# A decoder layer on one core: the first up-projection group also as seven products, and the norm's sums and scaling one group later

## The chip, the cores and the metric

The kernel runs on one core of one Trainium2 chip. The metric is the device time of one execution in microseconds; the median of several runs counts. Everything below is single-core, and the granted clock of the matrix engine in the profiled execution was 0.999 of full speed.

## The reference

One decoder layer on 512 tokens of width 1024, all in float32. Cut to what the change touches, the layer ends like this:

```python
x = x + jnp.einsum('bsd,de->bse', merged, w_out[l])        # 1024 x 1024
h2 = rmsnorm(x, norm_mlp_g[l])
up = jnp.square(jax.nn.relu(jnp.einsum('bsd,df->bsf', h2, w_up[l])))   # 1024 -> 4096
x = x + jnp.einsum('bsf,fd->bsd', up, w_down[l])           # 4096 -> 1024
```

Ahead of that lie a first RMS norm, one combined projection, differential attention, a gated linear recurrence and a gated merge of both branches. The change leaves their arithmetic alone.

## The kernel before, in words

**Splitting.** Each operand is split in two float32r parts: ScalarE copies it to `whi` (or the first half of an activation tile), VectorE subtracts that from the original and gets `wlo`. Every product is three matmuls: high by high, high by low, low by high. So each weight block of 128 x 1024 costs one DMA of 512 KB, one ScalarE cast and one VectorE subtraction before TensorE can use it. `cast_hi` and `cast_lo` (L1029 to L1057) do this for the last stage, `ahead` (L1059) calls them a step in advance. ScalarE and VectorE work strictly in the order in which the code issues their instructions (`InOrder`, L59).

**Weight buffers.** Four pairs `whi`/`wlo` go round, and every fifth unit of the last stage (L1035, `own`) has a pair of its own in the pool `fin`, which is opened when the pools of the middle stages close (L902). `fin` takes over their memory.

**The last stage** (L904 on) starts with the w_out projection in four pieces (`merged`, L929): each piece adds the residual into `x2`, multiplies with the gain into `q`, splits `q` into the tile `h2` (four forms), builds four sums of quarters (`sums`, L940, four more forms in `h2`), and squares `x2` for the norm. The norm's factor is not applied to `h2`: since relu squared passes it through, it is applied to `x2` instead.

**Up and down.** The 4096 hidden columns are cut into eight groups of 512. Odd groups (and, before the change, group 0) are computed plainly: kind `pl`, four weight blocks `b0`, `b2`, `b1`, `b3`, each block 24 matmuls of 512 columns. Groups 2, 4 and 6 are kind `up`: a 2 x 2 block product in seven products `M1` to `M7` (Winograd's form of Strassen), each 24 matmuls of 256 columns, in the order M1, M5, M6, M2, M7, M3, M4 (L957). M1, M6, M7 and M4 accumulate in one PSUM bank (Y), M5 and M3 in another (Z), M2 in a third (X); between them ScalarE or VectorE take the bank's state out (`up_out`, L1112): after M1 a copy `snap`, after M5 and M6 copies into `q`, after M2, M7 and M3 additions or subtractions. After every two groups come the seven products of the down projection, twice (kind `dn`). The list `steps` (L959 to L973) holds this order.

**Weight sums.** M5, M6, M7 and M4 of an `up` group need sums of weight blocks. `weight_sums` (L281) makes them on the DMA engines during the recurrence: GpSimd issues a load of one block into the tile `sum`, then a load that adds the next block, then a store to DRAM, ten DMAs a group one after another, since all go through the one tile. The tile lies in pool `stg`, at byte 225,248 to 229,344 of each partition. In `fin` the low half of the fifth unit's own pair (`wlo`) lies at 224,896 to 229,248, so the first instruction that writes it waits for the last of the weight sums' DMAs. In the kernel before, the fifth unit is block `b0` of group 1.

**The norm.** `sums2` (L1205) splits the sum of squares, `norm2` (L1208) adds it over the partitions with two matmuls, puts the result in `r2`, and schedules eight multiplications of `x2` with `r2`; they come before the first addition of a down product into `x2`. Calls put off by `later` run when a running estimate of TensorE's time (`tick`) has passed their due time.

Of the kernel before, what the change touches and what calls it, by code (L numbers as in the profile page):

```python
# [11 lines left out]
F32 = mybir.dt.float32  # L12
# [7 lines left out]
P = 128  # L20
# [17 lines left out]
def tile_block(ctx: ExitStack, tc: tile.TileContext, x, w_in, w_rga, w_rgx, w_pa, w_pr, w_o,  # L38
# [237 lines left out]
    tgr, tga = [None] * KT, [None] * KT  # L276
    es_act = ExitStack()
    stg = es_act.enter_context(tc.tile_pool(name="stg", bufs=1, side="right"))
    summed = [{p: dp.tile([P, 1024], F32, name=f"up{n}{p}") for p in ("M5", "M7", "M6", "M4")} for n in range(2, 8, 2)]

    def weight_sums(behind):  # L281
        t = stg.tile([P, 1024], F32, name="sum")
        G.tensor_copy(t[:, :1], behind[:, :1])
        for n in range(2, 8, 2):
            for blocks in (((0, None), (1, "M5"), (3, "M6"), (2, "M4")), ((1, None), (3, "M7"))):
                for b, p in blocks:
                    if p:
                        G.dma_start(t, w_up[n, b], accum_op=ALU.add)
                        G.dma_start(summed[n // 2 - 1][p], t)
                    else:  # L290
                        G.dma_start(t, w_up[n, b])

# [668 lines left out]
    def products(kind, a, order=ORDER7, first=3, lead=()):  # L961
        steps.extend((kind, a, p, q) for q in (range(first), range(first, 4)) for p in lead)
        steps.extend((kind, a, p, every) for p in order if p not in lead)

    I = InOrder(nc.tensor)
    for d in range(4):
        if d:
            products("up", 2 * d)
        else:
            products("pl", 0, ("b0", "b2", "b1", "b3"))  # L970
        products("pl", 2 * d + 1, ("b0", "b2", "b1", "b3"))
        products("dn", (d, 0))
        products("dn", (d, 1))  # L973
# [4 lines left out]
    for kind, a, p in ops:  # L978
        if kind == "pl":
            loads.append(((kind, a, p), w_up[a, int(p[1])]))  # L980
        elif kind == "up":
            loads.append(((kind, a, p), w_up[a, int(uses[p][0][1])] if p in ("M1", "M2", "M3") else summed[a // 2 - 1][p]))
# [76 lines left out]
    def ahead():  # L1059
        if half:  # L1060
            cast_lo()
        if can_cast():
            cast_hi()
# [11 lines left out]
    def later(us, f):  # L1075
        due.append((clk[0] + us, f))
# [128 lines left out]
    def sums2():  # L1205
        split(s2[:, 0], s2[:, 1], ssq)
# [10 lines left out]
    for j in range(4):  # L1217
        if j == 2:
            wb.raws = 2
        for n, _ in enumerate(merged(j)):  # L1220
            load()
            while late and n == 1:
                late.pop(0)()
            if j == 3 and n == 0:
                ahead()
                ahead()
            while owing and n == 0:
                owing.pop(0)()
    slots[0] += 1
    ahead()  # L1230
    ahead()
    owing.pop(0)()
    while late:
        late.pop(0)()
    later(3.0, owing.pop(0))
    later(6.0, lambda: late.pop(0)())
    seen, banks = {}, {}
    ACT8 = {"M1": 0, "M4": 3, "M2": 2, "M5": 4, "M6": 5, "M7": 6, "M3": 7}
    for n, (kind, a, p, pairs) in enumerate(steps):
        o = kind, a, p  # L1240
        if (kind, a) not in banks:
            banks[kind, a] = [psum("acc") for _ in range(4 if kind == "pl" else 3)]
            if kind == "dn" and a[0] == 3:
                banks[kind, a][1] = banks[kind, a][1], psum("acc")
        while n_low[0] <= number[o]:
            if half:
                cast_lo()
            else:
                assert can_cast()
                cast_hi()  # L1250
        hi, lo = units[number[o]]
        if kind == "pl":
            oc, kc = int(p[1]) % 2, int(p[1]) // 2
            ps = banks[kind, a][2 * oc:2 * oc + 2]
            for m in range(8):
                u, i = (m // 4, m % 4) if kc else (m % 2, m // 2)
                for e, (l, r) in enumerate(((hi, 0), (hi, 1), (lo, 0))):
                    I.matmul(ps[u], l[:, i, P * u:P * u + P], h2[:, r, i, 2 * kc:2 * kc + 2], start=kc == i == e == 0, stop=kc == 1 and i == 3 and e == 2)
                if m == 7:
                    finish(o)  # L1260
                if kc and i == 3:
                    plain_out(a, oc, u, ps[u])
                tick(0.68)
                if m % 4 == 3:
                    ahead()
            if n in (1, 3):
                sums2() if n == 1 else norm2()
            continue
        X, Y, Z = banks[kind, a]
        b = {"M2": X, "M5": Z, "M3": Z}.get(p, Y)  # L1270
        f = FORM[p]
        k = seen.get(o, 0)
        seen[o] = k + len(pairs)
        parts = [slice(u, u + 1) for u in range(2)] if isinstance(b, tuple) else [slice(0, 2)]
        if kind == "dn" and a[1] == 0 and p == "M1" and k == 0:
            I.matmul((b[0] if isinstance(b, tuple) else b)[:, :64], hi[:, 0, :P], forms[2 * a[0]][:, 0, f, 0, :64], start=True, stop=True)
        for u in range(2):
            d = b[u][:, :256] if isinstance(b, tuple) else b[:, 256 * u:256 * u + 256]
            for z, i in enumerate(pairs):
                for e, (l, r) in enumerate(((hi, 0), (hi, 1), (lo, 0))):  # L1280
                    act = h2[:, r, i, ACT8[p]] if kind == "up" else forms[2 * a[0] + i // 2][:, r, f, i % 2]
                    I.matmul(d, l[:, i, P * u:P * u + P], act, start=p in ("M1", "M2", "M5") and k == z == e == 0 and (u == 0 or isinstance(b, tuple)),
                             stop=i == 3 and e == 2, skip_group_check=True)
            if seen[o] == 4 and kind == "up" and u == 1:
                up_out(a, p, X, Y, Z)
            elif seen[o] == 4 and kind == "dn" and (len(parts) == 2 or u == 1):
                down_out(a, p, X, Y, Z, parts if len(parts) == 1 else parts[u:u + 1])
            if u == 0:
                tick(0.355 * len(pairs))
        if seen[o] == 4:  # L1290
            finish(o)
        if kind == "dn" and a[1] == 0 and p == "M2":
            if half:
                cast_lo(False)
        else:
            ahead()
        tick(0.355 * len(pairs))
# [43 lines left out]
```

## Time and profile before

| what | value |
|---|---|
| median of 3 runs | 856.3 us (854.63 to 857.79) |
| the profiled execution, its own time | 855.89 us |
| its span in the profile | 854.1 us |
| busy: TensorE / VectorE / ScalarE / GpSimd | 847.6 / 627.9 / 448.8 / 85.3 us |
| w_out projection | 486.95 to 530.46 us |
| groups 0 and 1, both plain, with the norm's two matmuls | 530.46 to 574.50 us |
| two down halves and group 2 | 574.50 to 631.90 us |
| group 3, plain | 631.90 to 653.70 us |

Times in the trace are counted from the start of the span. PE is TensorE, DVE is VectorE, ACT is ScalarE, POOL is GpSimd, SP the engine that issues most DMAs. Nearly every instruction goes through the helper of L67, so rows are told apart by tiles: `acc<-h,whi` is an up product, `acc<-us,whi` a down product. A busy time of PE counts overlapping records, so the time of one matmul in a stage is the stage's length over its number of matmuls.

### The profile page before, as it was taken

Reading aid. Unit: us, or ns where it says so; the run is one execution under the profiler, and the core shown is the slowest. Engines: PE = TensorE matmul, PEld = TensorE weight load, DVE = VectorE, ACT = ScalarE, POOL = GpSimd, SP = SyncE. Lnnn points to the kernel's source line nnn. Section 1 sums busy time; section 2 is a strip of 40 time slices with the busy share of each in tenths; the row PEclk is TensorE's granted clock in tenths of the full one; section 3 lists DMA queues with packets and bytes.
Section 4 is the critical chain, followed back from the end, with each engine's and each line's share of the span. In section 5 each row is a group of like instructions: output and inputs, shape, how many; then the busy total and the mean of one; then the engine's idle time right before and its main releaser. Section 6 shows DMA issues by size and latency. Waiting matters only on the chain.

```text
span 854.1 us, 13734 instructions
## 1 busy us (share of the span) xinstructions
PE 847.6 (99%) x5459; PEld 756.2 (89%) x5459; DVE 627.9 (74%) x1069; ACT 448.8 (53%) x703; POOL 85.3 (10%) x102
## 2 busy tenths in 40 slices
PE   9999999999999999999999999999999999999998
PEld 7899999999988887888888888889998998999898
DVE  6765688788865345878866767698787858776797
ACT  7444355544555334695673355654476357536642
POOL 0030222113111101011101100000000000000000
PEclk9999999999999999999999999999999999999999
DMA  6358222132231346757656671515752575456354
GB/s 201 122 163 239 91 69 87 39 111 63 66 103 43 87 135 196 196 173 209 165 157 196 207 263 50 172 25 149 214 179 54 155 237 148 124 150 197 99 143 129
DMA packets 38737, 119.76 MB, mean 140 GB/s; under 512 B 4609, under 2 KB 9417, under 8 KB 38673
## 3 DMA queue, kind: packets, MB, share of 16 engines
q1 hardware_dynamic: 31152, 92.65, 33.3%
q0 software_dynamic: 7520, 26.23, 13.8%
q8 instruction: 43, 0.70, 0.3%
q14 instruction: 22, 0.17, 0.1%
HBM read 102.05 MB, written 11.05 MB: 132 GB/s over the span
## 4 chain that ended last, share of the span: by engine, by line
PE 88%; DVE 5%; DMA 3%; ACT 2%; issue 1%; SPq 0%; ACTq 0%; DVEq 0%
PE acc L67 37%; PE acc L137 14%; PE acc L138 13%; PE acc L139 13%; DMA wraw<-in_w_in_dram 3%; PE at L564 2%; DVE wlo L67 2%; PE at L139 2%; PE at L137 2%; PE at L138 2%; ACT whi L67 1%; PE at L598 1%; PE at L516 1%; PE at L629 1%; DVE pe L67 1%
## 5 line engine op out<-in xcount | busy, mean ns | idle before, releaser
L67 PE MATMUL acc<-h,whi 128*128 128x512 f32 (+1 forms) x656 | 155.8, 331 | 0.0
L67 DVE TENSOR_TENSOR wlo<-wraw,whi 128x1024 fp32r<-128x1024 f32 (+2 forms) x86 | 96.9, 1149 | 78.1 <-ACT whi L67 78.0
L67 PE MATMUL acc<-us,whi 128*128 128x256 f32 (+1 forms) x900 | 153.2, 276 | 0.0
L67 ACT CAST whi<-raw 128x1024 fp32r<-128x1024 f32 x97 | 99.8, 1049 | 88.7 <-DVE raw L67 38.4
L67 PEld LDWEIGHTS acc<-us,whi 128*128 128x128 f32 x900 | 135.6, 188 | 0.4
L67 DVE TENSOR_TENSOR wlo<-raw,whi 128x1024 fp32r<-128x1024 f32 x97 | 117.6, 1219 | 13.6 <-ACT whi L67 13.4
L67 PE MATMUL acc<-us,wlo 128*128 128x256 f32 x448 | 123.7, 276 | 0.0
L67 PEld LDWEIGHTS acc<-h,whi 128*128 128x128 f32 x656 | 110.5, 188 | 12.3
L137 PE MATMUL acc<-whi,hT 128*128 128x256 f32 x384 | 109.9, 286 | 0.0
L67 PE MATMUL acc<-h,wlo 128*128 128x256 f32 (+1 forms) x328 | 108.6, 331 | 0.0
L67 ACT CAST whi<-wraw 128x1024 fp32r<-128x1024 f32 (+2 forms) x86 | 82.5, 981 | 48.1 <-DMA wraw<-in_w_in_dram 32.0
L138 PE MATMUL acc<-wlo,hT 128*128 128x256 f32 x384 | 107.4, 280 | 0.2 <-DVE wlo L67 0.2
L67 PEld LDWEIGHTS acc<-us,wlo 128*128 128x128 f32 x448 | 84.1, 188 | 0.0
L137 PE MATMUL acc<-hT,whi 128*128 128x512 f32 x208 | 82.2, 395 | 0.0
L139 PE MATMUL acc<-hT,wlo 128*128 128x512 f32 x208 | 81.0, 390 | 0.0
L139 PE MATMUL acc<-whi,hT 128*128 128x256 f32 x288 | 80.5, 279 | 0.0
L137 PEld LDWEIGHTS acc<-whi,hT 128*128 128x128 f32 x384 | 72.4, 189 | 4.3 <-issue 3.0
L138 PEld LDWEIGHTS acc<-wlo,hT 128*128 128x128 f32 x384 | 72.3, 188 | 1.0 <-issue 0.5
L67 ACT ACTIVATE pe<-pe,nm 128x128 f32<-128x128 f32 (+3 forms) x64 | 35.5, 556 | 66.0 <-DVE nm L67 66.0
L67 PEld LDWEIGHTS acc<-h,wlo 128*128 128x128 f32 x328 | 61.6, 188 | 6.3
L138 PE MATMUL acc<-hT,whi 128*128 128x512 f32 x156 | 60.9, 390 | 0.0
L67 POOL TENSOR_TENSOR rs<-ms,mhalf 128x8 f32<-128x8 f32 (+1 forms) x25 | 39.7, 1589 | 205.3 <-DVE ms L67 205.3
(205 smaller groups left out, 1625.3 us busy)
## 6 DMA issues: line engine op xcount, KB each, us to landing
wraw<-in_w_in_dram SPq DMA_DIRECT2D x54, 512.0 KB, 3.6
raw<-in_w_dn_dram SPq DMA_DIRECT2D x32, 512.0 KB, 4.4
raw<-in_w_up_dram SPq DMA_DIRECT2D x29, 512.0 KB, 4.1
sum<-in_w_up_dram POOLq DMA_DIRECT2D x18, 512.0 KB, 6.0
raw<-raw POOLq DMA_DIRECT2D x16, 512.0 KB, 4.6
wraw<-in_w_pa_dram SPq DMA_DIRECT2D x8, 512.0 KB, 4.6
wraw<-in_w_pr_dram SPq DMA_DIRECT2D x8, 512.0 KB, 4.6
wraw<-in_w_o_dram SPq DMA_DIRECT2D x8, 512.0 KB, 4.5
```

Source lines behind the costliest of these rows:

```text
L67: ins = f(*a, **k)
L137: T.matmul(o, l[0], r[0], start=first, stop=False)
L138: T.matmul(o, l[0], r[1], start=False, stop=False)
L139: T.matmul(o, l[1], r[0], start=False, stop=last)
L516: T.transpose(out=ps[:, t * P:(t + 1) * P], in_=qn[t // 2][:, c0:c0 + P], identity=ident)
L564: T.matmul(lg[c][:, :N], qT[r, x0, i * P:(i + 1) * P], kT[r, y0, :N], start=a == 0, stop=a == 2)
L598: T.transpose(out=tp[:, b * P:(b + 1) * P], in_=st[s][:, b * P:(b + 1) * P], identity=ident)
L629: T.matmul(ps[:, t:t + 1], sq[:, t * P:(t + 1) * P], ones, start=True, stop=True)
```

## The change

Group 0 becomes an `up` group as well: its weight sums are made first, in the same chain of DMAs, so that the chain has 40 DMAs in place of 30. In group 0 the products M1 and M5 are issued with their first three quarters of the contraction ahead, then the last quarter of each (`lead`), then the other five. The sums of quarters of the last piece of `merged` (`sums`) are issued at once after it, and the casts of the first units of the last stage move within that piece. `sums2` is called after M2 of group 0, `norm2` after block `b0` of group 1.

```diff
-    summed = [{p: dp.tile([P, 1024], F32, name=f"up{n}{p}") for p in ("M5", "M7", "M6", "M4")} for n in range(2, 8, 2)]
+    summed = [{p: dp.tile([P, 1024], F32, name=f"up{n}{p}") for p in ("M5", "M7", "M6", "M4")} for n in range(0, 8, 2)]
...
-        for n in range(2, 8, 2):
+        for n in range(0, 8, 2):
...
-                        G.dma_start(summed[n // 2 - 1][p], t)
+                        G.dma_start(summed[n // 2][p], t)
...
-        if d:
-            products("up", 2 * d)
-        else:
-            products("pl", 0, ("b0", "b2", "b1", "b3"))
+        products("up", 2 * d, lead=() if d else ("M1", "M5"))
...
-            if j == 3 and n == 0:
-                ahead()
+            if j == 3 and n in (0, 1, 2, 4, 6):
                 ahead()
             while owing and n == 0:
                 owing.pop(0)()
+    owing.pop(1)()
     slots[0] += 1
     ahead()
-    ahead()
-    owing.pop(0)()
     while late:
         late.pop(0)()
+    ahead()
     later(3.0, owing.pop(0))
-    later(6.0, lambda: late.pop(0)())
+    later(5.0, lambda: (late.pop(0)(), late.pop(0)()))
...
-            if n in (1, 3):
-                sums2() if n == 1 else norm2()
+            if a == 1 and p == "b0":
+                norm2()
...
+        if o == ("up", 0, "M2"):
+            sums2()
```

What this does to the order of the instructions is seen at two places. The first is TensorE where the w_out projection ends. The tiles `acc` are PSUM banks, `h2` holds the activations, `whi` and `wlo` the halves of a weight unit, and the brackets name whose semaphore is waited for. Before, group 0 begins with block `b0`:

```order
L139 MATMUL acc_5458<-mT_4916,wlo_5392 128x512
L67 MATMUL acc_5552<-h2_5215,whi_5465 128x512 [waits Activation_49]
L67 MATMUL acc_5552<-h2_5215,whi_5465 128x512
L67 MATMUL acc_5552<-h2_5215,wlo_5466 128x512 [waits DVE_49]
L67 MATMUL acc_5553<-h2_5215,whi_5465 128x512 x2
```

After the change the same place holds M1 (acc_5576) and M5 (acc_5577); shown are the start of M1, the last quarters of M1 and of M5, and the first matmul of M6, which goes into M1's bank:

```order
L67 MATMUL acc_5576<-h2_5229,whi_5479 128x256 [waits Activation_49]
...
L67 MATMUL acc_5576<-h2_5229,whi_5479 128x256 [waits DVE_49]
...
L67 MATMUL acc_5577<-h2_5229,whi_5502 128x256 [waits Activation_49]
L67 MATMUL acc_5577<-h2_5229,whi_5502 128x256 [waits DVE_49]
L67 MATMUL acc_5577<-h2_5229,wlo_5503 128x256
...
L67 MATMUL acc_5576<-h2_5229,whi_5526 128x256 [waits Activation_49]
```

The last quarters wait for the forms of `h2` that the last piece of `merged` makes, M5's for the sums of quarters, and M6 waits for ScalarE's copy of M1's bank.

The second place is VectorE at the same time: `fs` are the sums of quarters, `h2<-fs` their low half, `scratch` the norm's sums of squares. Before, the fifth unit's low half is `wlo_5572` (block `b0` of group 1), and it waits for two semaphores of GpSimd's DMAs (DMASW):

```order
L67 TENSOR_TENSOR wlo_5546<-raw_5316,whi_5545 128x1024 [waits DMAHW7_49]
...
L67 TENSOR_TENSOR fs_5577<-q_5527,fs_5577 128x256 [waits DVE_49]
L67 TENSOR_TENSOR wlo_5572<-raw_5469,whi_5571 128x1024 [waits DMASW5_49,DMAHW0_49,DMASW4_49,Activation_49]
L67 TENSOR_TENSOR h2_5215<-fs_5577,h2_5215 128x1024 [waits Activation_49]
L67 TENSOR_TENSOR wlo_5596<-raw_5537,whi_5595 128x1024 [waits DMAHW1_49,PE_49,Activation_49]
L67 TENSOR_TENSOR s2_5224<-scratch_5222,s2_5224 128x512 [waits Activation_49]
```

After the change the fifth unit is M7 of group 0 (`wlo_5573`); behind it stand the low halves of M3 (`wlo_5630`) and M4 (`wlo_5645`), the result of M2, the next group's first block and the result of M7 (`q_5628<-q_5628,acc_5576`):

```order
L67 TENSOR_TENSOR h2_5229<-fs_5559,h2_5229 128x1024 [waits Activation_49]
L67 TENSOR_TENSOR wlo_5566<-raw_5330,whi_5565 128x1024 [waits DMAHW7_49,Activation_49]
L67 TENSOR_TENSOR wlo_5573<-raw_5500,whi_5572 128x1024 [waits DMASW7_49,DMAHW0_49,DMASW6_49,Activation_49]
L67 TENSOR_TENSOR scratch_5236<-scratch_5236 128x512 [waits Activation_49]
L67 TENSOR_TENSOR scratch_5236<-scratch_5236 128x512 [waits DVE_49,Activation_49]
L67 TENSOR_TENSOR wlo_5630<-raw_5512,whi_5629 128x1024 [waits DMAHW1_49,PE_49,Activation_49]
L67 TENSOR_TENSOR wlo_5645<-raw_5542,whi_5644 128x1024 [waits DMAHW2_49,PE_49,Activation_49]
L67 TENSOR_TENSOR q_5628<-acc_5575,snap_5626 128x512 [waits PE_49]
L67 TENSOR_TENSOR s2_5238<-scratch_5236,s2_5238 128x512 [waits Activation_49]
L67 TENSOR_TENSOR wlo_5676<-raw_5570,whi_5675 128x1024 [waits DMAHW3_49]
L67 TENSOR_TENSOR q_5628<-q_5628,acc_5576 128x512 [waits PE_49]
```

The first sums of quarters moved up, ahead of all this, and the wait for the weight sums' last DMA moved from the second group's first block to the first group's fifth product.

More of the change, by code (lines that the diff above doesn't have):

```diff
@@ L981, in tile_block @@
         elif kind == "up":
-            loads.append(((kind, a, p), w_up[a, int(uses[p][0][1])] if p in ("M1", "M2", "M3") else summed[a // 2 - 1][p]))
+            loads.append(((kind, a, p), w_up[a, int(uses[p][0][1])] if p in ("M1", "M2", "M3") else summed[a // 2][p]))
         else:
```

## Prediction

> **What bounds the kernel now.** I read the page first, then TensorE's waits, then the stages by windows.
>
> ```profile
> PE 847.6 (99%) x5459; PEld 756.2 (89%) x5459; DVE 627.9 (74%) x1069; ACT 448.8 (53%) x703; POOL 85.3 (10%) x102
> ```
>
> The list of what TensorE waited for, complete:
>
> ```profile
> PE acc L67 <- DVE zero L67: 1.2, 1, 1.2
> PE at L137 <- ACT tt L67: 0.8, 1, 0.8
> PE at L598 <- DVE po L67: 0.2, 1, 0.2
> PE acc L138 <- DVE wlo L67: 0.2, 1, 0.2
> ```
>
> TensorE waits 2.4 us in 854.1 and nowhere after 530 us. So two things can move the time: fewer columns streamed through TensorE, and a new wait. The windows give the price of a matmul (in brackets the count; the second window holds two halves of the down product and group 2):
>
> ```profile
> 530.46:574.50 44.04, 44.04 (x195) 36.42 (x194) 34.68 (x45) 27.67 (x39) 0.89 (x1) 1.00 0.34 96
> 574.50:631.90 57.40, 57.40 (x506) 57.29 (x505) 46.65 (x54) 29.44 (x36) 2.60 (x3) 1.00 0.61 175
> ```
>
> The first window holds 194 matmuls of 512 columns (two groups of 96, two for the norm): 44.04 / 194 = 0.227 us each. The second holds 504 of 256 columns: 57.40 / 504 = 0.114 us each.
>
> **What is removed.** Group 0 costs 96 x 0.227 = 21.8 us; as seven products it costs 7 x 24 x 0.114 = 19.1 us. That is 2.7 us less if nothing waits. The reference mark is the end of group 0 without waits: 530.46 + 21.8 = 552.25 before.
>
> **First new wait: the last quarters.** M1 and M5 run three quarters each, then need the last piece's forms of the activations. TensorE reaches M1's last quarter 36 x 0.114 = 4.1 us and M5's 42 x 0.114 = 4.8 us after 530.46, at 534.6 and 535.2. VectorE's order in time around that point, before the change (x<-acc is the residual addition of the last piece, 503 to 506 us the sums of quarters of the first piece, for their durations):
>
> ```profile
> 503.04 0.42 DVE L67 TENSOR_TENSOR fs<-q 128x256 f32<-128x256 f32 x1
> 504.16 0.42 DVE L67 TENSOR_TENSOR fs<-q,fs 128x256 f32<-128x256 f32 x1
> 505.70 1.23 DVE L67 TENSOR_TENSOR h<-fs,h 128x1024 fp32r<-128x1024 f32 x1 [1.11 <-ACT h L67]
> 528.36 1.48 DVE L67 TENSOR_TENSOR scratch<-scratch 128x512 f32<-128x512 f32 x2
> 529.99 1.37 DVE L67 TENSOR_TENSOR x<-acc,x 128x512 f32<-128x512 f32 x2
> 532.65 1.29 DVE L67 TENSOR_TENSOR h<-q,h 128x512 fp32r<-128x512 f32 x2 [1.30 <-ACT h L67]
> 533.87 2.35 DVE L67 TENSOR_TENSOR wlo<-raw,whi 128x1024 fp32r<-128x1024 f32 x2
> 540.14 1.22 DVE L67 TENSOR_TENSOR wlo<-raw,whi 128x1024 fp32r<-128x1024 f32 x1
> ```
>
> In the new order three weight subtractions (M1, M5, M6) stand ahead of the additions, where one stood before, so the additions start 2.3 us later (the pair at 533.87), at 532.3. From there, by the same rows: 3.95 us to the end of the low halves (529.99 to 532.65 + 1.29), 1.5 us for the four sums (503.04 to 504.16 + 0.42), 1.1 us until ScalarE has copied them, 1.2 us for their low half. M5's last quarter gets its data at 532.3 + 7.8 = 540.1, 4.9 us after TensorE is there (with the old order it would be 2.6).
>
> **Second: M6 behind the copy of M1's bank.** On ScalarE that copy stands behind the copy of the sums (done at 538.9), two weight casts and two squares:
>
> ```profile
> 534.95 1.15 ACT L67 ACTIVATE scratch<-x 128x512 f32<-128x512 f32 x2
> 536.00 1.03 ACT L67 CAST whi<-raw 128x1024 fp32r<-128x1024 f32 x1
> 542.15 0.59 ACT L67 ACTIVATE q<-acc 128x512 f32<-128x512 f32 x1
> ```
>
> 538.9 + 2 x 1.03 + 1.15 + 0.6 = 542.7, while M5 ends at 540.1 + 5 x 0.114 = 540.7. M6 starts at 542.7, M2 follows, and TensorE is at M7 at 542.7 + 48 x 0.114 = 548.1, where without waits it would be at 530.46 + 96 x 0.114 = 541.4. These two waits alone cost 6.7 us, so the change would end 6.7 - 2.7 = 4.0 us slower.
>
> **Third, and last to end: M7's low half behind the weight sums.** It is the fifth unit; it overlaps the tile `sum` and waits for the last of the sums' DMAs. Before, the fifth unit's subtraction is the one at 540.14 us. After the change VectorE reaches it at about 541 (540.1 and one subtraction for M2). When is the tile free? GpSimd's issues, each DMA waiting for the one before:
>
> ```profile
> 320.53 0.54 POOL L67 DMA_DIRECT2D sum<-in_w_up_dram  x1 [0.30 <-POOL sum L67]
> 380.15 0.53 POOL L67 DMA_DIRECT2D sum<-in_w_up_dram  x1 [4.11 <-DMA up2M<-sum]
> 432.21 0.55 POOL L67 DMA_DIRECT2D up4M<-sum  x1 [8.71 <-DMA sum<-in_w_up_dram]
> 435.41 0.53 POOL L67 DMA_DIRECT2D sum<-in_w_up_dram  x1 [2.65 <-DMA up4M<-sum]
> 439.36 0.88 POOL L67 DMA_DIRECT2D sum<-in_w_up_dram  x1 [3.42 <-DMA sum<-in_w_up_dram]
> 452.30 0.87 POOL L67 DMA_DIRECT2D sum<-in_w_up_dram  x1 [2.64 <-DMA up6M<-sum]
> 457.80 0.55 POOL L67 DMA_DIRECT2D up6M<-sum  x1 [4.64 <-DMA sum<-in_w_up_dram]
> 487.81 0.55 POOL L67 DMA_DIRECT2D up6M<-sum  x1 [6.82 <-DMA sum<-in_w_up_dram]
> ```
>
> and what the trace says of the last group's stores, from issue to landing:
>
> ```profile
> DMA to landing us min/median/max: 2.9/4.4/9.2
> ```
>
> The 9.2 us belong to the store at 487.81, behind x's loads (the other three are followed sooner), so the tile is free at 497.0 us; the wait at 540 costs nothing before. Now a fourth group of ten DMAs follows from 497.0.
>
> Its bound from below is the fastest step of each kind: a load 3.95 us (435.41 to 439.36), an added load 5.5 (452.30 to 457.80), a store 3.2 (432.21 to 435.41). Two loads, four added loads and four stores: 7.9 + 22.0 + 12.8 = 42.7 us, so 539.7 at the earliest. The three groups took 59.6, 55.3 and 61.6 us; the longest would end at 558.6. What makes the difference is in the windows of the three groups and of the time after them (the last two columns are the DMA engines' share and GB/s):
>
> ```profile
> 320.50:380.20 59.70, 58.94 (x261) 48.47 (x260) 43.85 (x62) 37.51 (x52) 6.84 (x11) 1.00 0.66 186
> 380.20:435.40 55.20, 55.20 (x245) 45.73 (x244) 44.34 (x62) 37.20 (x54) 6.70 (x10) 1.00 0.67 185
> 435.40:497.00 61.60, 61.60 (x274) 51.00 (x273) 43.63 (x56) 24.77 (x32) 6.76 (x10) 1.00 0.71 209
> 497.00:506.00 9.00, 9.00 (x42) 7.44 (x41) 5.62 (x10) 4.82 (x7) 0.00 (x0) 1.00 0.84 325
> 506.00:530.00 24.00, 24.00 (x107) 19.88 (x106) 18.10 (x28) 13.44 (x20) 0.00 (x0) 1.00 0.21 66
> ```
>
> Moved bytes less ten times 0.524 MB of the sums' own leave 5.9, 5.0 and 7.6 MB, that is 11.2, 9.5 and 14.6 loads of 0.524 MB from SP's queue; the groups lasted 17.0, 12.5 and 18.9 us over 42.7. So each such load met on the way costs the chain 48.4 / 35.3 = 1.37 us. The fourth group meets 5.6 loads by 506 (9 us at 325 GB/s), two of the three that lie between 506 and 530 (24 us at 66 GB/s; the third is the fifth unit's, which now goes out later), then those of M7, M3 and M4, which go out as the low halves of M1, M5 and M6 are done (530 to 532), and one for group 1's first block: 11.6 x 1.37 = 15.9 us. I take off 1.0, since the queue that holds the first load up is empty by 506 + 1.6 (0.524 MB more at 325 GB/s). Together 42.7 + 14.9 = 57.6 us: the tile is free at 554.6. I take this value; both ends stay for the range.
>
> The Trainium skill, "DMA: Bandwidth & Descriptors", section "Anatomy of one DMA — SWDGE (gpsimd) path", gives 2.0 us plus bytes / 436 GB/s, an estimated 3.2 us for each of these DMAs; the trace agrees for the store alone (3.2) and has 5.5 for an added load. By that rule the fourth group would end at about 529 and the first two waits alone would count, 859.9 us.
>
> VectorE is in order, so while it waits from 541 to 554.6 the low halves of M3 and M4, the result of M2 and the norm's sums queue behind it. M7's subtraction ends at 555.8, TensorE goes on (it was at M7's third matmul at 548.4, so it waits 7.4 us there), M7 ends 22 x 0.114 = 2.5 us later, M3 2.7 us after that, at 561.0. M4 must wait until VectorE has taken M7's result out of its bank: after M7's low half come two norm sums 1.5, two subtractions 2.35, M2's result and the norm's low half 0.7 each (half a 128x1024 piece takes 1.29 / 2), one subtraction 1.2, and M7's result 0.7, that is 555.8 + 7.1 = 562.9. M4 ends at 565.6, against 552.25 for group 0 before: 13.3 us later.
>
> **What is left at nothing.** Three more units are cast on both engines and VectorE has three more bank results to take (3.5 + 2.1 us on VectorE): they are in the queue above or beside group 1. That group takes 21.8 us, and VectorE has some 7 us of gaps there before, so it should catch up as the down product begins; if not, each us that it is late there costs TensorE one. The norm's two matmuls only move. Its eight scalings (0.65 us each, as the halves above) now end after the down product begins and delay its first addition by about 1 us, which M5 (2.7 us) covers. Costs from below zero have no source here: no transfer and no column besides group 0's is dropped.
>
> **Sum.** 855.89 us for the profiled execution + 13.3 = 869.2; I say 869.0. That execution lies 0.4 us under the median of 856.3. A measurement of this kernel can tell about 0.5% from no change, 4.3 us: faster means below 852.0, slower above 860.6.
>
> **Rivals.**
> - *The weight sums end in time* (tile free by 545.3; above that each us costs one). The first two waits alone decide: 855.89 + 4.0 = 859.9, no change that can be told. For it: an unhindered chain ends at 539.7. Against it: each of the three groups took at least 12.5 us longer.
> - *Neither the sums nor the last quarters hold TensorE*, because VectorE and ScalarE run further ahead than I have it: 855.89 - 2.7 = 853.2. This is the other side, not slower. For it: TensorE waits for nothing in this stage before. Against it: from the last piece's end to its sums' low half there is a chain of 7 us that no order shortens below 2.6 us of waiting, and the tile's wait is in the program.
> - *The chain runs late*: at the longest group's 61.6 us the tile is free at 558.6 and the time is 855.89 + 17.3 = 873.2.
> - *The clock falls during the wait.* At the start of the trace, after idling, matmuls of 256 columns are slow:
>
> ```profile
> L67 PE MATMUL acc<-zero 128*128 128x256 f32 x17 | 4.0, 425 | 1.2 <-DVE zero L67 1.2
> ```
>
> 17 in 4.0 us is 0.235 us each, twice the 0.114. If the 7 us wait does that again for some 4 us, M7 and M3 take about 2 us longer; the wait for VectorE behind M7 covers most, so 869.0 to 871. The Trainium skill, "TensorE: Matmul & The Clock Gate", section "What you observe" and what follows, has the array at half rate after an idle window of about 3.4 us; no wait in this trace is long enough to show it.
>
> **How the numbers follow.** Forecast, 864 to 872: 0.62. Sums somewhat earlier, 860.6 to 864: 0.08. Late chain or clock, above 872: 0.10. Sums in time, about 859.9: 0.11. Nothing waits, about 853.2: 0.06, and 0.03 for a gain beyond 0.5% from something I have not seen. So slower 0.80, no change 0.17, faster 0.03. The range leaves out the 0.09 at the bottom and the upper 0.06: 859.0 to 873.0.
>
> **What would show it.** The profile after: GpSimd's last store of the sums issued near 551 and landing near 554.6; the list of TensorE's waits with one for VectorE's `wlo` of about 7 us and smaller ones for `h` and for ScalarE's copy; group 0 ending near 565; the stages from group 1 on unchanged in length. A last store landing before 545, or a wait for `wlo` under 1 us, would make the prediction wrong.

## The result, and the profile after

| | before | after |
|---|---|---|
| median | 857.04 us (854.63 to 858.41, 4 runs) | 868.97 us (866.87 to 872.6, 4 runs) |
| the profiled execution / its span | 855.89 / 854.1 us | 869.99 / 867.9 us |
| w_out projection begins | 486.95 | 489.22 |
| group 0 | 21.77 us | 29.51 us |
| group 1 with the norm's matmuls | 22.29 us | 22.32 us |
| first two down halves | 38.36 us | 39.78 us |
| group 2 / group 3 | 19.04 / 21.79 us | 19.04 / 21.79 us |
| second two down halves | 38.17 us | 39.89 us |
| group 4 | 19.04 us | 19.79 us |

The ratio is 1.0154 (95% interval 1.0123 to 1.0185): 11.9 us slower. The forecast number, 869.0, was met, but by chance: of the two mechanisms that it was built on, one did not happen. In the profiled executions the spans differ by 13.7 us: 7.7 in group 0, 1.4 + 1.7 in the two down stages, 0.75 in group 4, and 2.3 ahead of w_out, before the fourth group's first DMA goes out at 488.25 (w_out begins anywhere from 486.2 to 491.2 in the runs below); the rest gives 0.2 back.

The first line of the page, and the list of TensorE's waits from the end of w_out to the start of the down product:

```profile
PE 853.1 (98%) x5531; PEld 763.1 (88%) x5531; DVE 632.4 (73%) x1075; ACT 453.2 (52%) x707; POOL 92.2 (11%) x112
```

```profile
PE acc L67 <- ACT h L67: 2.2, 1, 2.2
PE acc L67 <- DVE wlo L67: 2.0, 1, 2.0
PE acc L67 <- ACT snap L67: 1.3, 1, 1.3
PE acc L67 <- ACT us L67: 0.9, 1, 0.9
PE acc L67 <- DVE h L67: 0.9, 1, 0.9
```

Before, nothing waited here. Four of these waits lie in group 0 (`us` belongs to the down product). The 7.4 us for `wlo` that the forecast put at M7 are not there: the 2.0 us for `wlo` are M1's. Group 0, cut where TensorE's granted clock (the column after the busy times) changes, with the stage of the down product below it:

```profile
532.74:536.40 3.66, 1.70 (x14) 1.50 (x13) 3.56 (x5) 1.44 (x2) 0.89 (x1) 1.00 0.30 41
536.40:539.90 3.50, 3.50 (x19) 3.50 (x19) 2.14 (x4) 1.91 (x4) 0.49 (x1) 0.51 1.01 282
539.90:546.70 6.80, 2.86 (x20) 2.27 (x19) 5.65 (x9) 4.50 (x7) 0.07 (x1) 1.00 0.56 224
546.70:550.10 3.40, 2.92 (x13) 2.92 (x14) 3.29 (x5) 2.81 (x4) 0.00 (x0) 0.50 0.76 257
550.10:562.25 12.15, 12.15 (x109) 12.15 (x108) 8.18 (x10) 8.45 (x11) 0.00 (x0) 1.00 0.58 188
sum 29.51, PE 23.14 PEld 22.34 DVE 22.82 ACT 19.11 POOL 1.44; mean PE 4.63 PEld 4.47 DVE 4.56 ACT 3.82 POOL 0.29
...
584.57:643.40 58.83, 57.86 (x507) 57.46 (x505) 49.50 (x60) 30.03 (x37) 2.60 (x3) 1.00 0.56 170
```

Group 0's 168 matmuls need 19.04 us. TensorE is idle for 29.51 - 23.14 = 6.4 us (the four waits), and busy 4.1 us too long. Of these, 2.8 are the two stretches at half clock: 32 matmuls in 3.50 + 2.92 us, where 32 x 0.114 = 3.65 would do. The down stage with group 2 takes 58.83 us, 57.40 before.

GpSimd's issues of the fourth group of weight sums, its first and its last, and how long the last one took from issue to landing:

```profile
488.25 0.53 POOL L67 DMA_DIRECT2D sum<-in_w_up_dram  x1 [5.97 <-DMA up4M<-sum]
...
539.41 0.56 POOL L67 DMA_DIRECT2D up6M<-sum  x1 [4.88 <-DMA sum<-in_w_up_dram]
...
DMA to landing us min/median/max: 6.2/6.2/6.2
```

So the tile is free at 539.4 + 6.2 = 545.6 us.

VectorE at the hand-over: the residual additions of the last two pieces, the low halves, the forms of the last piece:

```profile
524.75 1.28 DVE L67 TENSOR_TENSOR x<-acc,x 128x512 f32<-128x512 f32 x2
...
533.82 3.49 DVE L67 TENSOR_TENSOR wlo<-raw,whi 128x1024 fp32r<-128x1024 f32 x3
537.22 1.28 DVE L67 TENSOR_TENSOR x<-acc,x 128x512 f32<-128x512 f32 x2
539.87 1.29 DVE L67 TENSOR_TENSOR h<-q,h 128x512 fp32r<-128x512 f32 x2 [1.36 <-ACT h L67]
...
543.74 1.23 DVE L67 TENSOR_TENSOR h<-fs,h 128x1024 fp32r<-128x1024 f32 x1 [1.11 <-ACT h L67]
544.88 2.35 DVE L67 TENSOR_TENSOR wlo<-raw,whi 128x1024 fp32r<-128x1024 f32 x2
```

The pair at 544.88 is M2 and M7, back to back: M7's subtraction, the one that waits for the last of the sums' DMAs, begins at about 546.0, 0.4 us after the tile is free, and does not wait. The forecast had VectorE there at 541. The last additions stand at 537.22, where the forecast had them at 532.3 (or 534.6, with this execution's later w_out). Counted from w_out's start they are at 48.0 us; before, at 529.99 - 486.95 = 43.0. Where these 5 us begin is seen on ScalarE, whose cast of a w_out weight block waits for the load. After, and before:

```profile
506.17 1.05 ACT L67 CAST whi<-wraw 128x1024 fp32r<-128x1024 f32 x1 [3.39 <-DMA wraw<-in_w_o_dram]
```

```profile
500.81 1.05 ACT L67 CAST whi<-wraw 128x1024 fp32r<-128x1024 f32 x1 [0.31 <-DMA wraw<-in_w_o_dram]
```

The load lands 3.1 us later, counted from w_out's start: at 16.9 us (issued at 8.8) where it was at 13.8 (issued at 6.5) before. So 2.3 of the 3.1 us were there when it was issued, and SP's loads of x, which come ahead of it, were 2.5 us later as well. How much of this is the fourth group's traffic can't be read from this pair of executions. The w_out projection as a whole, before and after (the last two columns are the DMA engines' share and GB/s):

```profile
486.95:530.46 43.51, 43.51 (x193) 36.03 (x192) 30.27 (x46) 21.51 (x30) 0.55 (x1) 1.00 0.51 179
```

```profile
489.22:532.74 43.52, 43.52 (x194) 36.05 (x192) 29.62 (x45) 21.73 (x31) 4.81 (x7) 1.00 0.81 253
```

### The profile page after: what moved, and what is told of

The parts are those of the page before. It is cut to its first block, busy times and chain, and to the rows that moved or that the text cites. A ratio compares the mean times of both kernels' runs of the same rounds, so it can differ in the third digit from the quotient of the medians.

```text
span 867.9 us, 13910 instructions
## 1 busy us (share of the span) xinstructions
PE 853.1 (98%) x5531; PEld 763.1 (88%) x5531; DVE 632.4 (73%) x1075; ACT 453.2 (52%) x707; POOL 92.2 (11%) x112
## 4 chain that ended last, share of the span: by engine, by line
PE 68%; DVE 12%; ACT 8%; DMA 7%; issue 3%; SPq 0%; ACTq 0%; DVEq 0%
PE acc L67 31%; PE acc L137 10%; PE acc L138 9%; PE acc L139 9%; DMA wraw<-in_w_in_dram 5%; DVE wlo L67 4%; ACT whi L67 4%; PE at L564 2%; PE at L139 1%; ACT q L67 1%; PE at L137 1%; PE at L138 1%; DVE fs L67 1%; PE at L598 1%; DMA wraw<-in_w_o_dram 1%
## 5 line engine op out<-in xcount | busy, mean ns | idle before, releaser
L67 PE MATMUL acc<-h,whi 128*128 128x256 f32 (+1 forms) x704 | 159.4, 323 | 4.4 <-ACT h L67 2.2
L67 ACT CAST whi<-raw 128x1024 fp32r<-128x1024 f32 x100 | 102.6, 1050 | 87.8 <-DVE raw L67 38.0
L67 DVE TENSOR_TENSOR wlo<-raw,whi 128x1024 fp32r<-128x1024 f32 x100 | 121.1, 1220 | 16.9 <-ACT whi L67 16.8
L67 PEld LDWEIGHTS acc<-h,whi 128*128 128x128 f32 x704 | 118.0, 192 | 14.8 <-ACT h L67 2.4
L67 PE MATMUL acc<-h,wlo 128*128 128x256 f32 (+1 forms) x352 | 113.3, 322 | 2.0 <-DVE wlo L67 2.0
L67 PEld LDWEIGHTS acc<-h,wlo 128*128 128x128 f32 x352 | 67.7, 192 | 7.2 <-DVE wlo L67 2.2
```

Of the source, the lines that this page charges most:

```text
L67: ins = f(*a, **k)
```

## The experiments

Theories at the start: the waits for the last piece's forms with the half clock behind them (mine, once the trace was read); the weight sums' last DMA, as forecast; the traffic of the fourth group; VectorE's and ScalarE's extra work, whatever the data dependence; and the norm's move for the loss in the down stage.

| run | median, us | ratio to before (95%) | group 0, us |
|---|---|---|---|
| after | 868.97 | 1.0154 (1.0123 to 1.0185) | 29.51 |
| three groups of sums | 866.4 | 1.0110 (1.0080 to 1.0140) | 26.86 |
| sums early | 867.33 | 1.0127 (1.0103 to 1.0151) | 28.82 |
| no last sums | 868.59 | 1.0149 (1.0112 to 1.0187) | 30.29 |
| before, four groups of sums | 859.29 | 1.0031 (1.0014 to 1.0049) | 26.77 (plain) |
| before, norm later | 857.87 | 1.0016 (1.0004 to 1.0028) | 21.77 (plain) |
| mended order | 871.1 | 1.0173 (1.0157 to 1.0189) | 27.20 |
| mended order, sums early | 874.32 | 1.0208 (1.0190 to 1.0226) | 28.38 |
| filling matmuls | 863.94 | 1.0086 (1.0068 to 1.0104) | 28.26 with 5.0 of filling |
| norm back | 868.45 | 1.0121 (1.0083 to 1.0160) | 31.23 |
| filling, norm back | 864.42 | 1.0083 (1.0060 to 1.0105) | 26.57 with 5.0 of filling |
| no last quarter | 868.47 | 1.0128 (1.0099 to 1.0157) | 31.82 |
| before, norm later, two wide matmuls | 856.99 | 1.0005 (0.9993 to 1.0016) | 21.77 (plain) |

### Three groups of sums

```diff
-        for n in range(0, 8, 2):
+        for n in range(0, 6, 2):
...
-            loads.append(((kind, a, p), w_up[a, int(uses[p][0][1])] if p in ("M1", "M2", "M3") else summed[a // 2][p]))
+            loads.append(((kind, a, p), w_up[a, int(uses[p][0][1])] if p in ("M1", "M2", "M3") else summed[a // 2 % 3][p]))
```

> The changed kernel with a chain of 30 DMAs: group 6 uses group 0's weight sums in place of its own (so its products are of the wrong weights). Contention theory: the extra ten DMAs hold up the loads of x and the weights in the w_out stage, so VectorE comes late to M1's low half; without them the 2.0 us wait for that half and the first half-clock spell (1.7 us) go, and up to 1 us ahead of the stage: 864 to 865.5 us. The prediction's theory (the fifth unit waits for the chain's end): the chain ends near 490, that wait goes, 860 us. If only the order of work inside group 0 counts: 869 us, no change.

Measured: 866.4 us, 2.6 less than after, though the intervals of the two ratios overlap. The last store was issued at 480.34, no w_out block was waited for, and VectorE's last additions came 44.7 us after w_out's start:

```profile
531.30 1.28 DVE L67 TENSOR_TENSOR x<-acc,x 128x512 f32<-128x512 f32 x2
```

M1's low half was in time, the waits for `h` and for the copy stayed, and one stretch of 6.8 us ran at half clock. This execution is the fastest of four (863.8 to 868.91). With the ratio still at 1.0110, most of the loss is there without any fourth group.

### Sums early

```diff
-                if j == 0:
-                    weight_sums(d[0]["xc"])
...
+    weight_sums(ident)
```

> The changed kernel with all four groups of sums, but the chain issued right after attention, about 28 us earlier, so that it ends near 516 us. Contention theory: much like the run with 30 DMAs, 864 to 866 us. Prediction's theory: 860 us. Order inside group 0 alone: 869 us. If the collisions only move to the recurrence: 869 us with new waits of TensorE near 300 to 330 us.

Measured: 867.33 us. The last store goes out at 510.85, 28.6 us ahead of the one after the change:

```profile
510.85 0.55 POOL L67 DMA_DIRECT2D up6M<-sum  x1 [5.04 <-DMA sum<-in_w_up_dram]
```

and the time hardly moves. So the wait for the weight sums is not what costs. The cast of a w_out block waited 2.2 us here too.

### No last sums

In group 0 the last quarter of every product reads the last piece's plain forms in place of its sums of quarters.

```diff
-                    act = h2[:, r, i, ACT8[p]] if kind == "up" else forms[2 * a[0] + i // 2][:, r, f, i % 2]
+                    act = h2[:, r, i, ACT8[p] % 4 if a == 0 and i == 3 else ACT8[p]] if kind == "up" else forms[2 * a[0] + i // 2][:, r, f, i % 2]
```

> The changed kernel, but in group 0 the last quarter of M5, M6, M7 and M3 reads the last piece's plain forms in place of its sums of quarters (so these products are wrong); the sums are still made. Order theory: M5's waits for the sums (2.2 and 0.9 us) go, and with them the second half-clock spell (1.7 us) if the copy of M1's bank is not as late by itself: 864 to 866 us. Contention theory alone: 869 us. Prediction's theory (the wait is at M7): 869 us.

Measured: 868.59 us, as after. TensorE's waits, in place of the 2.2 for `h`:

```profile
PE acc L67 <- ACT snap L67: 5.0, 1, 5.0
PE acc L67 <- DVE wlo L67: 2.3, 1, 2.3
```

Taking the data away moved the wait to the next thing in ScalarE's queue, the copy of M1's bank.

### Before, four groups of sums

```diff
-    summed = [{p: dp.tile([P, 1024], F32, name=f"up{n}{p}") for p in ("M5", "M7", "M6", "M4")} for n in range(2, 8, 2)]
+    summed = [{p: dp.tile([P, 1024], F32, name=f"up{n}{p}") for p in ("M5", "M7", "M6", "M4")} for n in range(0, 8, 2)]
...
-        for n in range(2, 8, 2):
+        for n in range(0, 8, 2):
```

> The kernel before with the chain of 40 DMAs: group 0's sums are made and not used. Contention theory: the w_out stage starts 1 to 2 us later and the last piece's additions come late, but group 0 as plain products hides that: 857.5 to 859.5 us. Prediction's theory: the fifth unit, here group 1's first block, is needed at 552 and the chain ends at 543 to 555: 857 to 861 us, with a wait for wlo at group 1 if late. Order theory: 857 us, no change.

Measured: 859.29 us, 2.7 more by the ratio (1.2 to 4.2). Nobody reads the fourth group's sums, so what is left of the change is its traffic and the later end of the chain. In the profiled execution, which is the slowest of ten (858.26 to 862.38), group 0, still plain, took 26.77 us in place of 21.77: 2.6 us of waiting for the last piece's `h` and a stretch of 3.4 us at half clock. It begins with the same row on ScalarE:

```profile
506.86 1.05 ACT L67 CAST whi<-wraw 128x1024 fp32r<-128x1024 f32 x1 [5.19 <-DMA wraw<-in_w_o_dram]
```

Here VectorE did wait for the chain's end, before the low half of the fifth unit (block `b0` of group 1), but this comes after the waits above, and TensorE waited for nothing behind it:

```profile
548.47 1.23 DVE L67 TENSOR_TENSOR wlo<-raw,whi 128x1024 fp32r<-128x1024 f32 x1 [2.45 <-DMA up6M<-sum]
```

### Before, norm later

```diff
-            if n in (1, 3):
-                sums2() if n == 1 else norm2()
+            if n == 1:
+                sums2()
+            if a == 1 and p == "b0":
+                norm2()
```

> The kernel before with only the norm's move: its two matmuls and eight scalings after block b0 of group 1 in place of the end of group 0. If the scalings make VectorE late for the down product: the first two down halves take 39.5 to 40 us in place of 38.4 and the run 858 to 858.8 us. If the lateness after the change comes from group 0 instead: no change within 0.5%, 857 us, down halves 38.4 us.

Measured: 1.4 us by the ratio (0.3 to 2.4). The first down halves take 39.97 us and group 2 takes 19.79, with no wait in TensorE's list:

```profile
574.48:614.45 39.97, 39.89 (x338) 39.67 (x337) 33.44 (x43) 18.98 (x23) 2.60 (x3) 1.00 0.57 159
614.45:634.24 19.79, 19.79 (x171) 19.79 (x170) 15.40 (x14) 11.21 (x14) 0.00 (x0) 1.00 0.58 186
```

The clock is full. 19.79 / 168 is 0.1178 us a matmul where 19.04 / 168 is 0.1133: every matmul is 4.4 ns slower, from about 580.6 us, after short hesitations at 578.3 and 580.5 (the longest step between two starts is 0.455 us), to the next group of 512 columns.

### Mended order, and the same with the sums early

M2 joins M1 and M5 in running three quarters ahead, and the copy of M1's bank goes ahead of the next casts and the squares. The second kernel adds the early sums.

```diff
-        products("up", 2 * d, lead=() if d else ("M1", "M5"))
+        products("up", 2 * d, lead=() if d else ("M1", "M5", "M2"))
...
-    ahead()
...
-    ahead()
-    later(3.0, owing.pop(0))
-    later(5.0, lambda: (late.pop(0)(), late.pop(0)()))
+    later(7.2, owing.pop(0))
+    later(8.0, lambda: (late.pop(0)(), late.pop(0)()))
...
-        if o == ("up", 0, "M2"):
+        if o == ("up", 0, "M2") and seen[o] == 4:
             sums2()
...
-        else:
+        elif n >= 3:
             ahead()
```

> The changed kernel with group 0's order mended: M2 also runs three quarters ahead (2 us more work before the sums of quarters are needed), and ScalarE copies M1's bank before the casts for M6 and M7 and before the squares. Order theory: waits for the sums of quarters and the copy fall from 4.4 us to about 1 us and one half-clock spell goes: group 0 in 24 to 26 us in place of 29.5, the run 864 to 865 us. Contention theory alone: 868 to 869 us. Prediction's theory (fifth unit behind the chain): 869 us, with a wait for wlo of the fifth unit.

> The mended order and the chain of sums 28 us earlier. Contention and order together: M1's low half comes in time as well, group 0 in 20 to 23 us, the run 860 to 862 us. Order theory alone: like the run with the mended order only. If neither: 867 us.

Measured: 871.1 and 874.32 us, worse than after. Group 0 falls to 27.20 and 28.38, but the first down halves take 44.71 and 45.79 us, with a half-clock stretch of their own:

```profile
579.67:624.38 44.71, 41.45 (x338) 40.26 (x337) 36.87 (x48) 21.77 (x28) 2.60 (x3) 0.96 0.52 146
```

ScalarE has 28 instructions in these halves, where it has 23 after the change. So the work that was put off in group 0 comes due here, and is late here.

### Filling matmuls

44 matmuls of 256 columns, 14 ahead of M1 and 30 ahead of its last quarter, into a bank that nobody reads.

```diff
+    spare_bank = psum("acc")
+
+    def idle_work(count):
+        for _ in range(count):
+            I.matmul(spare_bank[:, :256], h2[:, 0, 0, 0, :P], h2[:, 0, 0, 1], start=True, stop=True)
...
+        if n in (0, 2):
+            idle_work(14 if n == 0 else 30)
```

> The changed kernel with 14 extra matmuls of 256 columns before M1 and 30 before M1's last quarter, into a bank of their own that nobody reads: 5.0 us more work on TensorE, put where it waits. If the two spells at half clock (2 x 1.7 us) come from these waits, they go, and the waits of 5 to 6 us take in the extra work: 865 to 867 us. If the clock plays no part and the extra work only fills waits: 869 to 870 us. If the waits do not cover it: 873 us.

Measured: 863.94 us. With 44 x 0.114 = 5.0 us of useless work the kernel is 0.7% faster than after, by ratios whose intervals don't meet. In the profiled execution the clock stays full through group 0:

```profile
530.75:540.76 10.01, 9.63 (x81) 9.43 (x80) 8.48 (x13) 3.90 (x6) 0.89 (x1) 1.00 0.74 198
540.76:559.00 18.24, 15.84 (x134) 15.22 (x133) 14.52 (x16) 15.28 (x20) 0.55 (x1) 1.00 0.69 229
```

In the profiled executions, from w_out's start to the end of the span, it saves 3.4 us: 1.25 in group 0, 1.4 in the second down stage and 0.75 in group 4, which keep the faster step here.

### Norm back, alone and with the filling

```diff
-            if a == 1 and p == "b0":
-                norm2()
...
+        if o == ("up", 0, "M4") and seen[o] == 4:
+            norm2()
```

> The changed kernel with the norm's two matmuls and its scaling called at the end of group 0 again, as before the change; the sums are still split after M2. Theory: the norm's later scaling puts VectorE late as the down product begins and costs 1 to 2 us there, so the first two down halves go from 39.8 back to about 38.4 us and group 2 stays at 19.04; the time is 867 to 868. Rival: the down stage is late because of the casts and bank results left over from group 0, whatever the norm does; then the down halves stay at 39.5 or more and the time is 869 or above. Group 0 itself should stay at 29 to 30 us in both.

> The changed kernel with 44 filling matmuls (14 ahead of M1, 30 ahead of its last quarter, into a bank that nobody reads) and the norm called at the end of group 0 again. Theory, both losses being independent: 863.9 less 1 to 2 for the norm, so 862 to 863, group 0 at 28.3 with the filling, the first two down halves at 38.4. It would still be slower than before, by 5 to 6 us, since the waits for the last piece's forms are only filled and not removed. Rival, that the work left over sets the down stage: 864 with the down halves at 39.5 or more.

Measured: 868.45 and 864.42 us, no difference from after and from the filling alone that the intervals could show. In the profiled executions the stage itself did what the theory said in both: the first down halves and group 2 take 57.21 us, where they take 58.83 after and 58.79 with filling alone, and TensorE's wait for `us` is gone:

```profile
586.01:643.22 57.21, 57.21 (x507) 57.21 (x505) 46.74 (x54) 29.28 (x36) 2.59 (x3) 1.00 0.59 175
```

With the norm back alone, group 0 was 1.7 us longer than after in these executions, which eats it; why the gain doesn't show with the filling stays open. The second down stage took 39.62 us there and 38.17 with the filling, so what slows that one is not the norm.

### No last quarter

```diff
-                    act = h2[:, r, i, ACT8[p]] if kind == "up" else forms[2 * a[0] + i // 2][:, r, f, i % 2]
+                    act = h2[:, r, 2 if a == 0 and i == 3 else i, ACT8[p]] if kind == "up" else forms[2 * a[0] + i // 2][:, r, f, i % 2]
```

> The changed kernel, but the last quarter of each of group 0's seven products reads the third piece's activations in place of the last piece's; the last piece's forms are made as before and not read in group 0. So this leaves out the dependence on the last piece and keeps every cast, sum and DMA. Theory (the waits for the last piece's forms, and the half clock that follows them, make the loss): group 0 falls from 29.5 to 20 to 23 us, with waits for M1's low half and for the copy of M1's bank alone, no half clock, and the time is 858 to 862. Rival (VectorE and ScalarE cannot keep up with the seven units' casts, whatever the last piece does): group 0 stays above 27 us and the time above 866.

Measured: 868.47 us, group 0 31.82. My theory falls and the rival stands, though the last piece's forms are still made here, and how much of the queue is theirs and how much is the casts' isn't separated. Without any dependence on the last piece, TensorE waits for M1's low half and for the copy of M1's bank:

```profile
PE acc L67 <- ACT snap L67: 4.2, 1, 4.2
PE acc L67 <- DVE wlo L67: 4.2, 1, 4.2
```

M5's last matmul starts at 542.97 us here, six after M1's last, which so starts at 542.3; but ScalarE comes to the copy only after the last piece's forms, two casts and two squares:

```profile
542.99 1.04 ACT L67 CAST h<-fs 128x1024 fp32r<-128x1024 f32 x1 [2.31 <-DVE fs L67]
543.94 1.99 ACT L67 CAST whi<-raw 128x1024 fp32r<-128x1024 f32 x2
545.83 1.14 ACT L67 ACTIVATE scratch<-x 128x512 f32<-128x512 f32 x2
546.88 0.56 ACT L67 COPY snap<-acc 128x512 f32<-128x512 f32 x1
```

### Two wide matmuls in the down stage

The kernel before with the norm later, and two matmuls of 512 columns behind the third product of the first down half (M6), into a bank that nobody reads.

```diff
+        if o == ("dn", (0, 0), "M6"):
+            spare_bank = psum("acc")
+            for z in range(2):
+                I.matmul(spare_bank, h2[:, 0, z, 0, :P], h2[:, 0, z, 0:2], start=z == 0, stop=z == 1)
```

> The kernel before with the norm one group later, as in the run with that change alone, and two matmuls of 512 columns into a bank that nobody reads behind M6 of the first down half (about 588 us). It measures the slower step alone: there the stream of 256-column matmuls ran at 117.8 ns each from 578 us until the plain group at 634. Theory: a matmul of 512 columns resets the step, so from 588 us it is 113.3 again, the first two down halves take about 38.9 us with the 0.46 us of the two matmuls, and group 2 takes 19.04. Rival: the step depends on something else of that stage (the DMAs, the other engines' reads); then group 2 takes 19.79 and the halves 40.4.

Measured: 856.99 us, not to be told from before. The down stage ahead of the two matmuls, and after them with group 2:

```profile
574.53:583.40 8.87, 8.79 (x74) 8.57 (x73) 8.74 (x16) 6.41 (x10) 0.88 (x1) 1.00 0.32 62
583.87:613.80 29.93, 29.93 (x266) 29.93 (x264) 24.24 (x28) 12.11 (x13) 1.72 (x2) 1.00 0.65 190
613.80:632.84 19.04, 19.04 (x171) 19.04 (x169) 15.30 (x14) 11.11 (x14) 0.00 (x0) 1.00 0.62 195
```

29.93 / 264 is 0.1134 us: the wide matmuls end the slower step, as the theory said. The halves took 39.28 us with them, 0.4 more than I had put; the 72 matmuls ahead took 8.87 us, where 8.16 would do at 0.1133.

### What decides group 0

For the kernels that keep the order of before or of the change and have no filling, one number of the profiled execution goes with the length of group 0: how long after w_out's start VectorE begins the last piece's residual additions. Each row is one execution.

| run | ScalarE idle for the w_out block cast in the second piece, us | last additions after w_out's start, us | group 0, us |
|---|---|---|---|
| before | 0.31 | 43.0 | 21.77 (plain) |
| before, four groups | 5.19 | 47.7 | 26.77 (plain) |
| three groups of sums | none | 44.7 | 26.86 |
| sums early | 2.21 | 46.7 | 28.82 |
| after | 3.39 | 48.0 | 29.51 |
| no last sums | 3.76 | 48.4 | 30.29 |
| norm back | 3.59 | 49.0 | 31.23 |
| no last quarter | 3.99 | 50.2 | 31.82 |

From 44.7 to 50.2 the seven-product group grows by 5.0 us over 5.5, nearly one for one, and the two kernels with less to wait for in the data lie on the same line. The plain group grows by 5.0 us over 4.7. The third column follows the second to within 1.5 us: the new order alone puts the additions 1.6 us later (44.7 against 43.0), and what a w_out block is late comes on top. All ten kernels with four groups of sums waited 1.5 us or more for that block (1.50 with the mended order), which landed 15.0 to 19.1 us after w_out's start; the four with three groups waited 0.31 at most, and it landed at 10.8 to 13.8. So the lateness of ScalarE and VectorE at the hand-over sets group 0, and not one dependence behind them: two runs took a dependence away and gained nothing, and three changed the chain alone (three groups, sums early, before with four) and moved the additions and group 0 together. What isn't shown is how the 9.4 us (1.0110) that are left with three groups divide between the casts, the sums of quarters and the last piece's forms, since no run made that work smaller.

## Why the prediction was right or wrong

- **What is removed: right.** 168 matmuls at 0.1133 us are 19.04 us, shown wherever nothing waits, against 21.8.
- **The first two waits: right in sum, not in form.** They were put at 6.7 us, and TensorE was idle for 6.4; that these agree is luck. 2.0 of them are M1's low half, which the forecast had in time; the last quarters waited 3.1 (put at 4.9) and M6 1.3. The additions were put at 532.3 because only the three subtractions ahead of them were counted (2.3 us, measured 1.6 with three groups). That VectorE and ScalarE would be 3.3 us later still than with three groups, behind a w_out load that was late in every kernel with four, was not in it. The forecast priced what loads from SP's queue do to the sums' chain, and never what the chain does to those loads.
- **The third wait: wrong.** This is the step that failed. The fourth group was put at 497.0 to 554.6. It ran from 488.25 to 545.6. The length was right (57.4 us, 57.6 forecast); the start was not. It was taken from one execution, and the third group's last store varies with the run: issued at 487.81 before, 474.54 and 472.56 in two other kernels with the same chain. And VectorE came to M7's subtraction at 546.0 in place of 541, so that what was left of the wait (4.6 us, or 2.3 counted from this execution's later w_out) went as well: the two errors together made it nothing. Of the forecast's own two signs of being wrong, a last store landing before 545 is missed by 0.6 us, and a wait for `wlo` under 1 us is met for M7's.
- **The rival "the weight sums end in time" is what happened**, but its price of 859.9 was not. It left out three things that the runs show. TensorE was busy 4.1 us longer in group 0, 2.8 of them the half clock, where the clock rival had 2 us and let a wait cover them. The slower down stages and group 4: 1.4 + 1.7 + 0.75. The start of w_out: 2.3 us, which were lost before the fourth group began; eight of the ten kernels with four groups began w_out later than all four with three (486.6 to 487.0), in one execution each, so it isn't shown that this is chance. 859.9 + (4.1 - 0.3) for group 0 + 3.9 + 2.3 is 869.9, the profiled execution's time. The number 869.0 was met by luck: these stand where the 9.3 us of M7's wait and the queue behind it had stood.
- **The norm at nothing: wrong by 1 to 2 us.** Moving it alone in the kernel before costs 1.4 us (0.3 to 2.4), and moving it back inside the change brings the first down stage from 58.83 to 57.21 in the trace, though the run's time doesn't show it. The forecast saw the later scaling and took M5 to cover it. In the kernel before, what costs is mostly the slower step that a hesitation leaves behind: with two wide matmuls that end it, 0.4 us is left (-0.6 to 1.4; the two runs' intervals overlap, the traces tell them apart). After the change it is the hesitation itself, the wait for `us` within it: group 2 ran at the faster step, 19.04 us.
- **"VectorE should catch up as the down product begins": right, but for the norm.** After the change VectorE stands idle for 5.74 us of group 1, from 562.7 us on, so it has worked off its queue by then:

```profile
568.43 0.69 DVE L67 TENSOR_TENSOR fs<-q 128x512 f32<-128x512 f32 x1 [5.74 <-issue]
```

The wait of 0.9 us for `us` at the down product is not in the list of either run with the norm back. (Of the 7 us of gaps that the forecast counted in group 1 before, more than half lie ahead of it: in group 1's 22.26 us VectorE was busy for 19.31.) Only the mended orders, which leave more over, lost 4.9 us and more against the change at that place.
- **Open:** what slows the second down stage after the change (39.89 us; 38.17 with filling and norm back, 38.50 with no last quarter), how much of the 2.7 us that four groups cost the plain kernel and of the 2.6 us in the changed one is the same for every execution, and how the rest of group 0's loss divides among the work at the hand-over.

## What to carry to other kernels

An engine that nobody waits for may still have no slack: here VectorE and ScalarE were just in time at one hand-over, and each us that they came later cost TensorE about one. Price added DMA traffic in both directions, also for the loads that it delays, and don't take the end of a long chain from one execution. Where a wait is removed, read the in-order queue of the engine that ended it: if the next thing that TensorE needs stands behind the same instructions, nothing is gained.

## What the runs showed of the hardware that was not expected

After the change TensorE's clock fell to half for 3.4 us at a time (6.8 in several other runs), after waits of 2.0 and 2.2 us, none longer. The Trainium skill, "TensorE: Matmul & The Clock Gate", section "HAM oscillation — how this bites in real kernels", asks for no idle gap over about 3.4 us; here shorter ones were enough. What the traces show is the share of a fixed window. The half-clock stretches begin and end on one grid of 3.41 us; here are three of its windows after the change, the first and the third right ahead of a half-clock stretch:

```profile
533.03:536.44 3.41, 1.45 (x12) 1.35 (x12) 3.31 (x5) 1.15 (x2) 0.89 (x1) 1.00 0.31 40
...
539.86:543.27 3.41, 1.67 (x15) 1.47 (x13) 2.73 (x6) 1.11 (x2) 0.11 (x1) 1.00 1.03 411
543.27:546.68 3.41, 1.24 (x6) 0.84 (x6) 2.94 (x3) 3.41 (x6) 0.00 (x0) 1.00 0.10 41
```

TensorE was busy for 0.43 and 0.36 of the windows before a fall, and for 0.49 of the one that was followed by full clock. In the fourteen traces all 28 falls, half of them as the kernel ends, follow a window busy for 0.47 or less, and no full-clock window with 0.49 or more is followed by one (one with 0.44, at the end of the mended order, isn't either). Useless matmuls in the waits kept the clock full: with them no window of group 0 was busy for less than 0.63.

A stream of 256-column matmuls has two steady rates at full clock, 0.1133 and 0.1178 us each. After a hesitation it can run at the slower one for more than 50 us, until 512-column matmuls come; in the one run that tried it, two of those, 0.47 us, restored the faster. A hesitation doesn't always do it: after the same wait of 0.9 us for `us`, group 2 ran at 19.04 us after the change and at 19.79 with the sums early. What decides is open.
